# A decoder layer on one core: two feed-forward chunks by seven products, and more weight remainders by transfer

## The chip, the cores and the metric

The kernel runs on one NeuronCore of a Trainium2 chip. The metric is device time in microseconds (us) of one execution. TensorE (PE, with its weight loads as PEld), VectorE (DVE), ScalarE (ACT), GpSimd (POOL) and SyncE (SP) each run their own list of instructions in the order written. They wait for each other through semaphores. SP, ACT and POOL can issue DMA transfers.

## The reference

One decoder layer on 256 tokens of width 1024, in float32. The part that the change touches is the last one, with D_FF = 2816:

```
def swiglu(h, w_gate, w_up, w_down):
    return (jax.nn.silu(h @ w_gate) * (h @ w_up)) @ w_down
...
        mix = jnp.concatenate([pool_out, attn_out], axis=-1) @ w_out[l]
        h = layer_norm(DEEPNORM_ALPHA * h + mix, ln1_g[l], ln1_b[l])
        h = layer_norm(DEEPNORM_ALPHA * h + memory_cross_attention(h, mem, w_xq[l], w_xkv[l], w_xo[l]),
                       ln2_g[l], ln2_b[l])
        h = layer_norm(DEEPNORM_ALPHA * h + swiglu(h, w_gate, w_up, w_down), ln3_g[l], ln3_b[l])
```

## The kernel before

**Numbers in two parts.** A float32 operand is held as a high part (rounded to TensorE's reduced float32) and a low part (the rest). A product of two operands is three matmuls: high x high, high x low, low x high (`three`). A weight tile of 128 x 1024 numbers (0.524 MB) is loaded by SP into a raw page. ACT casts the high part from it, and DVE subtracts to get the low part (`split`). For a tile named in `BY_DMA`, `parted` does otherwise: ACT writes the negated high part into the low page, and POOL issues a DMA that adds the weight from DRAM onto it. Names such as w63 are weight tiles in the order of their making; r, h and l behind a name are raw, high and low.

**Stages.** The layer runs through input projections, attention and pooling, keys of the memory (xk), the output projection (mix), the values of the memory (xv), the queries (xq), the output of the cross attention (xo), gate and up (gu), down (d), and the last norm. DFF is cut into 11 chunks of 256 columns. Chunk 0 is formed in rows: the token rows stand on the partitions, 48 matmuls of 512 columns, then SiLU and product, then four transposes. Chunks 1 to 10 are formed the other way round (`proj_both`): 32 matmuls of 512 columns and 32 of 256, and the result needs no transpose. `gated` adds the two accumulators, applies SiLU and product, splits the result and, for the down stage, forms four sums of its quarters (`add_sums`) and splits these.

**Seven products instead of eight.** `Blocks.seven` multiplies a 256 x 256 operand by a 256 x 1024 weight in seven block products rather than eight, from the quarters and four sums of quarters on both sides. That is 21 matmuls of 512 columns, three for each of the seven. The sums of the weight's quarters are made in one of three ways, which a letter names. 'D' loads both rows and adds on DVE (`FromVector`). 'S' adds in DRAM ahead of time: copies and adds by DMA into sumt, mixt or xot, then loads of the sums (`FromDram`). 'A' loads two quarters and lets POOL add two others onto them in SBUF by DMA, and DVE adds the other two sums (`FromAdded`). A weight pair has tiles o (the first quarter, shared by two pairs), y (two quarters), z and w (two sums each). `MIX`, `XO` and `DOWN` give the letter of each pair of a stage. The sums take the bank accumulators 1 to 7; `joined` and the adds behind it put the four output quarters together. `several` and `DEFER` put the last pairs' last three products at the end.

**The order.** `Plan.schedule` fixes the order of every engine before the program is built. TensorE's order is the order of the code. The others are filled by deadlines worked back from TensorE's nominal times, with a model of durations and of the transfer queue. Tiles take slots: 42 pages of 4 KB per partition, 4 big ones, 8 halves. A load may be issued only when a slot is free, and `MARGIN`, `SPARE`, `RAWS` say how far ahead slots may be taken. `LEAVE` is the time after which a bank should be empty, `PATIENCE` how long an engine may hold back for a more urgent operation. `XV_STEPS` and `XA_STEPS` say after how many products of xv, xq and xo the transposes and attention steps stand. `transpose_tok` transposes half a row of tokens and splits it into h1T or h2T, the operands of the next stage. `APART` says, for each half of token block 0 in the last norm, whether ACT and POOL scale it (`scale_apart`) or DVE (`scale`).

## Time and profile before

| what | value |
|---|---|
| median of 3 runs | 371.98 us (371.61 to 373.33) |
| the profiled execution | 373.54 us, of which the span 371.6 us |
| PE busy | 363.6 us, 98% of the span |
| DVE busy | 320.2 us, 86% |
| ACT busy | 242.6 us, 65% |
| POOL busy | 38.2 us, 10% |
| DMA moved | 95.26 MB, 256 GB/s over the span |

The span reaches from the first to the last instruction of the profiled execution. Busy is the time in which an engine has an instruction under way. A matmul's duration overlaps that of the next one, so what a product costs is read from the distance of starts, not from its duration. The same holds, by less, for passes of DVE. The DMA share in the windows is the mean busy share of 16 DMA engines; it can be a little over 1 since packets overlap.

### The profile page before, as it was taken

What the parts mean: (1) busy time and instruction counts of PE and PEld (TensorE: products, weight loads), DVE (VectorE), ACT (ScalarE), POOL (GpSimd) and SP (SyncE); (2) the same over time, 40 slices, a digit from 0 to 9 for tenths busy, and PEclk for the clock granted to TensorE, in tenths of its full rate; (3) what the DMA queues carried; (4) which work ended last, traced back from release to release, by engine and by line L of the source; (5) the groups of instructions that cost most, each with busy time, mean ns of one, the idle gap of its engine ahead of it and who ended that gap; (6) DMA issues with size and microseconds to landing.
All of it is one profiled execution on the core that took longest, in us unless ns stands there. A gap on an engine that the chain in (4) does not pass through costs nothing. (4 is left out here: it accounts for less than half of the span.)

```text
span 371.6 us, 5494 instructions
## 1 busy us (share of the span) xinstructions
PE 363.6 (98%) x1971; PEld 310.9 (84%) x1971; DVE 320.2 (86%) x489; ACT 242.6 (65%) x364; POOL 38.2 (10%) x43
## 2 busy tenths in 40 slices
...
GB/s 225 415 417 416 335 305 300 82 196 197 305 408 353 201 220 297 52 304 323 330 319 372 284 278 361 294 259 181 221 275 59 217 95 227 282 267 417 52 0 113
DMA packets 34059, 95.26 MB, mean 256 GB/s; under 512 B 3440, under 2 KB 5488, under 8 KB 34032
## 3 DMA queue, kind: packets, MB, share of 16 engines
...
q0 software_dynamic: 6688, 12.85, 20.1%
...
q10 hardware_dynamic: 288, 0.33, 0.2%
...
## 5 line engine op out<-in xcount | busy, mean ns | idle before, releaser
L528 DVE TENSOR_TENSOR sg<-banks,sg 128x512 f32<-128x512 f32 x20 | 12.9, 685 | 14.9 <-ACT sg L510 14.9
L510 ACT COPY sg<-banks 128x512 f32<-128x512 f32 x20 | 10.7, 587 | 18.7 <-PE banks L571 18.7
L1362 POOL TENSOR_TENSOR rs<-rs,mhalf 128x1 f32<-128x1 f32 x6 | 5.6, 930 | 46.9 <-DVE rs L542 46.9
L533 DVE SCALAR_TENSOR_TENSOR r<-r,mv,g 128x512 f32<-128x512 f32 (+2 forms) x12 | 8.3, 720 | 0.0
L533 DVE SCALAR_TENSOR_TENSOR r<-r,rs,b 128x512 f32<-128x512 f32 (+1 forms) x10 | 6.8, 707 | 1.3 <-POOL rs L1362 1.2
L1350 DVE BATCH_NORM_STATS2 st<-r 128x6 f32<-128x512 f32 (+1 forms) x12 | 7.7, 665 | 0.2
L518 ACT ACTIVATE xpr<-banks,mx 128x256 f32<-128x256 f32 x8 | 3.7, 470 | 6.4 <-DVE mx L890 6.4
L559 POOL DMA_DIRECT2D sumt<-in_s_down x4 | 4.2, 1040 | 35.1 <-DMA sumt<-in_s_down 35.1
L528 DVE TENSOR_TENSOR sg<-sg 128x512 f32<-128x512 f32 x10 | 6.8, 685 | 0.7 <-ACT sg L518 0.7
L518 ACT ACTIVATE sg<-sg 128x512 f32<-128x512 f32 x10 | 6.4, 635 | 1.3 <-DVE sg L528 1.3
L518 ACT ACTIVATE pr<-pr,mx 128x128 f32<-128x128 f32 (+1 forms) x16 | 7.1, 451 | 0.0
L528 DVE TENSOR_TENSOR r<-banks,r 128x512 f32<-128x512 f32 (+1 forms) x11 | 7.0, 655 | 0.0
L510 ACT CAST rest<-r 128x256 fp32r<-128x256 f32 x1 | 0.4, 407 | 9.6 <-DVE r L528 9.6
L559 POOL DMA_DIRECT2D mixt<-in_s_out x2 | 2.5, 1240 | 38.9 <-DMA mixt<-in_s_out 38.9
L518 ACT ACTIVATE pr<-pr,sm 128x256 f32<-128x256 f32 (+1 forms) x16 | 5.8, 447 | 0.0
L576 PEld LDWEIGHTS banks<-ident,r 128*128 128x128 f32 x32 | 3.9, 140 | 1.5 <-DVE r L533 0.6
L576 PE MATMUL banks<-ident,r 128*128 128x128 f32 x32 | 4.8, 273 | 0.2 <-DVE r L533 0.2
L533 DVE SCALAR_TENSOR_TENSOR xql<-banks,xq 128x512 f32<-128x512 f32 x4 | 2.8, 690 | 2.5 <-ACT xq L518 2.5
L913 DVE CUSTOM_DVE_ANT_0 pr<-banks,tri 128x128 f32<-128x128 f32 (+1 forms) x16 | 4.7, 352 | 0.2
L510 ACT CAST h1T<-banks 128x512 fp32r<-128x512 f32 x4 | 2.3, 587 | 3.8 <-PE banks L576 3.8
L518 ACT ACTIVATE xq<-banks 128x512 fp32r<-128x512 f32 x4 | 2.4, 593 | 3.7 <-PE banks L571 3.7
L559 POOL DMA_DIRECT2D w47l<-in_w_gu x1 | 1.2, 1237 | 30.8 <-ACT w47l L518 30.8
...
## 6 DMA issues: line engine op xcount, KB each, us to landing
...
mixt<-in_s_out SPq DMA_DIRECT2D x3, 512.0 KB, 8.9
g<-in_ln_g SPq DMA_DIRECT2D x3, 512.0 KB, 7.4
b<-in_ln_b SPq DMA_DIRECT2D x3, 512.0 KB, 7.3
...
mr<-in_mem_t SPq DMA_DIRECT2D x2, 512.0 KB, 10.5
mixt<-in_s_out POOLq DMA_DIRECT2D x2, 512.0 KB, 12.7
xt<-in_x SPq DMA_DIRECT2D x2, 512.0 KB, 4.2
```

The source lines that it names most:

```text
L510: return self.add(eng, lambda: f(out.ap(), src.ap()), out, [src], 1, **kw)
L518: nc.scalar.activation(out.ap(), src.ap(), func, bias=val(bias), scale=val(scale), **more)
L528: return self.add(eng, lambda: e.tensor_tensor(out.ap(), a.ap(), b.ap(), op=op), out, [a, b], 2, **kw)
L533: return self.add(eng, lambda: e.scalar_tensor_tensor(out.ap(), a.ap(), val(scalar), b.ap(), op0=op0, op1=op1), out, [a, b, scalar], 2, **kw)
L559: return self.plan.op("POOL", lambda: self.nc.gpsimd.dma_start(val(out), val(src), accum_op=OP.add, max_dma_last_dim=2048), [out], [src], ...
L576: return self.plan.op("PE", lambda: self.nc.tensor.transpose(ps.ap(), src.ap(), ident.ap()), [ps], [src, ident], 0.109, DRAIN, kind=False)
L913: nc.vector.tensor_tensor_reduce(o.ap(), i.ap(), tri.ap()[:, S - w:], -1.0, -NEG, op0=OP.add, op1=OP.min, accum_out=m.ap())
L1350: plan.op("DVE", lambda: nc.vector.bn_stats(st.ap(), r.ap()), [st], [r], *kit.cost("DVE", c1 - c0))
L1362: plan.op("POOL", lambda: nc.gpsimd.tensor_tensor(rs.ap(), rs.ap(), mhalf.ap(), op=OP.pow), [rs], [rs, mhalf], 0.83, 0.05)
```

## The change

The change forms chunks 4 and 5 of gate and up together (`group`, step 'G0' of `SEQUENCE`): their 512 gate and 512 up columns are one weight of 1024 x 1024, four pairs of 256 rows, each in seven products by the way 'A', with sums of h2's quarters on the other side. For these `transpose_tok` keeps a raw copy of h2T (h2raw, two pages, copied by ACT), and `form_of_h2` makes and splits the sums (hs). The result comes out in rows, and is transposed. Chunk 6 is formed in rows (step 'R6'), and the eight transposes of chunks 4 and 5 stand in it; its own four stand in chunk 7. `gated_t` now also forms the sums of quarters from a copy.

In the other stages the letters D of the mix and S of xo and down become A, so that nothing of down and xo is added in DRAM any more. `BY_DMA` lists thirty names instead of nine. The second half of token block 0 in the last norm goes to DVE. The planner gets other constants and, in its model of the transfers, a list of times at which SP's queue is held up; `XV_STEPS`, `XA_STEPS` and `IN_BIG` change. Of the new code's `AHEAD` nothing runs, since it is 0. The core of the diff:

```diff
-LEAVE = 3.0
-PATIENCE = 0.7
-MARGIN, SPARE, RAWS = 100.0, 1, 6
+LEAVE = 2.0
+PATIENCE = 1.0
+MARGIN, SPARE, RAWS = 40.0, 1, 5
 BEHIND = 1.35
 RING = 256
-ADD_LATE = 6.0, 100.0
+AHEAD = 0.0
+FETCHES = 18.9, 43.5, 62.5, 82.0, 110.0, 137.0, 154.0, 179.5, 205.0, 226.5, 248.0, 268.5, 290.0, 313.0, 343.5
+ADD_LATE = (6.0, 100.0)
...
-MIX = ('D', 'D', 'S', 'S')
+MIX = ('A', 'A', 'S', 'S')
 VAL = ('', '', '', '')
-XO = ('D', 'S', '', '')
-DOWN = {1: 'A', 2: 'A', 3: 'S', 4: 'S', 5: 'A', 6: 'A', 7: 'S', 8: 'S', 9: 'A'}
+XO = ('D', 'A', '', '')
+DOWN = {1: 'A', 2: 'A', 3: 'A', 4: 'A', 5: 'A', 6: 'A', 7: 'A', 8: 'A', 9: 'A'}
 LAST = tuple(c for c in range(NFC) if c not in DOWN)
-BY_DMA = ('w27', 'w28', 'w29', 'w36', 'w47', 'w49', 'w52', 'w56', 'w59')
-DEFER = (1, 2)
-APART, HALF_STORES = (True, True), True
-IN_BIG = ('g1', 'g2')
+BY_DMA = ('d4o', 'd6o', 'd7y', 'd8o', 'd8y', 'gu0y', 'gu1y', 'gu2y', 'w27', 'w28', 'w30', 'w33', 'w36', 'w37', 'w47', 'w49', 'w52', 'w57', 'w61', 'w73', 'w75', 'w78', 'w81', 'w83', 'w88', 'w91', 'w93', 'w95', 'xo1o', 'xo1y')
+DEFER = (1, 2, 1)
+GROUPS = ((4, 5),)
+TURN_AT = (1, 2)
+SEQUENCE = (1, 2, 3, 'G0', 'R6', 7, 8, 9, 10)
+APART, HALF_STORES = (True, False), True
+IN_BIG = ('g1', 'g3')
...
-XV_STEPS = 16, 4
-XA_STEPS = ((21, 's0'), (34, 'p0'), (35, 's1'), (52, 'p1'), (52, 's2'), (53, 'a0'), (59, 'a1'), (61, 'p2'), (69, 's3'), (73, 'a2'), (77, 'p3'))
+XV_STEPS = (12, 6)
+XA_STEPS = ((21, 's0'), (34, 'p0'), (37, 's1'), (53, 's2'), (53, 'a0'), (56, 'p1'), (58, 'p2'), (60, 'a1'), (68, 's3'), (75, 'a2'), (77, 'p3'))
...
-        split(*gated_parts(0), pt.re("p f (t s) -> p (f t) s", t=T))
+                kit.transpose(pt[:, f, t * P:(t + 1) * P], rows_[t][:, f * P:(f + 1) * P], ident)
+        q = pt.re("p f (t s) -> p (f t) s", t=T)
+        hl = gated_parts(c)
+        if c not in LAST:
+            raw = half("sg", [4, P], hold=12)
+            copy("ACT", raw, q)
+            q = raw
+            add_sums((hl[0][:, 4:8], hl[1][:, 4:8]), q)
+        split(hl[0][:, 0:4], hl[1][:, 0:4], q)
...
+            three(ps, h2T.pair(k, slice(t * P, (t + 1) * P)), c_gu[c].get(k), k == 0, k == KD - 1)
             yield
+    h2_sums = {}
+    def form_of_h2(j):
+        if j not in h2_sums:
+            v = h2_sums[j] = page(f"hs{j}", [2, 4, P], F32R)
+            add_sums((v[:, 0], v[:, 1]),
+                     h2raw[j // 2][:, 2 * (j % 2):2 * (j % 2) + 2, :].re("p k (t s) -> p (k t) s", t=T))
+        def get(f):
+            if f < 4:
+                return h2T.pair(2 * j + f // 2, slice(f % 2 * P, (f % 2 + 1) * P))
+            return h2_sums[j][:, 0, f - 4], h2_sums[j][:, 1, f - 4]
+        return get
+    gu_sums = DramSums("gu", s_gu, y_gu, 4 * len(GROUPS), 0) if GROUPS else None
+    def group(n):
+        b = Blocks("gm")
+        yield from b.several([(form_of_h2(j), FromAdded(f"gu{4 * n + j}", gu_sums, 4 * n + j), "A", 0) for j in range(4)],
+                             DEFER[2], ORDERS, None)
+        m1, u2, u3 = b.joined()
+        g = [half("gr", [512], hold=12) for _ in range(2)]
+        u = [half("ur", [512], hold=8) for _ in range(2)]
+        tt("DVE", g[0], b.m[2], m1, OP.add)
+        tt("DVE", u[0], b.m[5], u2, OP.subtract)
+        tt("DVE", u[1], b.m[5], u3, OP.subtract)
+        tt("DVE", u[0], b.m[3], u[0], OP.add)
+        tt("DVE", g[1], b.m[4], u3, OP.add)
+        for y, z in zip(g, u):
+            act(y, y, AF.Silu)
+            tt("DVE", y, y, z, OP.mult)
+        turned.extend((c, [y[:, i * CW:(i + 1) * CW] for y in g]) for i, c in enumerate(GROUPS[n]))
...
+    for at, c in enumerate(SEQUENCE, 1):
         mark = [plan.pe[-1]]
-        if c <= len(thirds):
-            down_sums.begin(thirds[c - 1], mark)
-        if c == 3:
+        if at <= len(thirds):
+            down_sums.begin(thirds[at - 1], mark)
+        if at == 3:
             for js in thirds:
                 down_sums.add(js, mark)
-        gu = proj_both(pss + more, c_gu[c], h2T, KD if c < NFC - 3 else 2)
-        if c == 1:
-            run(gu, 8)
-            gated_t()
-        run(gu)
-        gated(c, gate, up)
+        if isinstance(c, str) and c[0] == "G":
+            g = group(int(c[1:]))
+            if turned:
+                run(g, 4)
+                turn()
+            run(g)
+        elif isinstance(c, str):
+            c = int(c[1:])
+            before = list(turned)
+            turned.clear()
+            for t in range(T):
+                row = bank("pg")
+                g = rows_of(c, t, row)
+                if t == TURN_AT[0]:
+                    run(g, TURN_AT[1])
+                    for other, rows_ in before:
+                        gated_t(other, rows_)
+                run(g)
+                gated_row(c, t, row)
+            turned.append((c, [sg_rows[c][:, t, :] for t in range(T)]))
+        else:
+            gate, pss = two("pg")
+            up, more = two("pu")
+            gu = proj_both(pss + more, c_gu[c], h2T, KD if at < len(SEQUENCE) - 2 else 2)
+            if turned:
+                run(gu, 8)
+                turn()
+            run(gu)
+            gated(c, gate, up)
+    turn()
```

On TensorE, at the place of chunk 4, this is the order before: eight products of each weight tile with h2T, high parts first.

```order
L571 MATMUL banks<-h2T_2050,w62l 128x256 x8
L571 MATMUL banks<-h2T_2032,w63h 128x512 x8
L571 MATMUL banks<-h2T_2032,w64h 128x512 x8
L571 MATMUL banks<-h2T_2050,w65h 128x512 x8
L571 MATMUL banks<-h2T_2050,w66h 128x512 x8
L571 MATMUL banks<-h2T_2032,w63l 128x256 x8
L571 MATMUL banks<-h2T_2032,w64l 128x256 x8
```

At the same place after: the group's tiles gu0y, gu0o, gu0z and gu0w against quarters of h2T and their sums hs.

```order
L600 MATMUL banks<-h2T_2043,w62l 128x256 x8
L600 MATMUL banks<-gu0yh,h2T_2019 128x512
L600 MATMUL banks<-gu0yl,h2T_2019 128x512
L600 MATMUL banks<-gu0yh,h2T_2019 128x512
L600 MATMUL banks<-gu0yh,hs_2234 128x512
L600 MATMUL banks<-gu0yl,hs_2234 128x512
L600 MATMUL banks<-gu0yh,hs_2234 128x512
L600 MATMUL banks<-gu0oh,h2T_2019 128x512
L600 MATMUL banks<-gu0ol,h2T_2019 128x512
L600 MATMUL banks<-gu0oh,h2T_2019 128x512
L600 MATMUL banks<-gu0zh,hs_2234 128x512
```

The two chunks' 64 matmuls each are replaced by 84 of 512 columns, every one in three behind the tiles of its pair.

On VectorE, around the sums of chunk 3's product (sg), the order before: low parts of later weight tiles between.

```order
L528 TENSOR_TENSOR w76l<-w76r,w76h 128x1024
L528 TENSOR_TENSOR sums<-sg 128x256
L528 TENSOR_TENSOR g3l<-sg,g3h 128x512
L528 TENSOR_TENSOR sums<-sums,sg 128x128
L528 TENSOR_TENSOR w77l<-w77r,w77h 128x1024
L528 TENSOR_TENSOR sums<-sg,sums 128x128
L528 TENSOR_TENSOR w78l<-w78r,w78h 128x1024
L528 TENSOR_TENSOR w79l<-w79r,w79h 128x1024
```

At the same place after:

```order
L557 TENSOR_TENSOR gu3w<-gu3y,gu3z 128x512
L557 TENSOR_TENSOR sums<-sg 128x256
L557 TENSOR_TENSOR gu3w<-gu3y,gu3w 128x512
L557 TENSOR_TENSOR sums<-sums,sg 128x128
L557 TENSOR_TENSOR sums<-h2raw_2047 128x256
L557 TENSOR_TENSOR g_2534<-sg,g_2534 128x512
L557 TENSOR_TENSOR sums<-sg,sums 128x128
L557 TENSOR_TENSOR sums<-sums,h2raw_2047 128x128
L557 TENSOR_TENSOR gu3zl<-gu3z,gu3zh 128x1024
L557 TENSOR_TENSOR sums<-h2raw_2047,sums 128x128
L557 TENSOR_TENSOR gu3wl<-gu3w,gu3wh 128x1024
L557 TENSOR_TENSOR gu3yl<-gu3y,gu3yh 128x1024
```

Where low parts of tiles four chunks ahead stood, the group's last tiles are made ready, and the first of these rows needs POOL's add into gu3z.

On POOL, the adds for the down stage before (the other sums came from DRAM, added earlier into sumt):

```order
L559 DMA sumt_101<-sumt_100 128x512
L559 DMA d1z<-in_s_down 128x2x512
L559 DMA d2z<-in_s_down 128x2x512
L559 DMA d5z<-in_s_down 128x2x512
L559 DMA d6z<-in_s_down 128x2x512
L559 DMA d9z<-in_s_down 128x2x512
```

And after, nine sums and three low parts (yl, w83l) of the same stage:

```order
L588 DMA d1z<-in_s_down 128x2x512
L588 DMA d2z<-in_s_down 128x2x512
L588 DMA d3z<-in_s_down 128x2x512
L588 DMA d4z<-in_s_down 128x2x512
L588 DMA d5z<-in_s_down 128x2x512
L588 DMA d6z<-in_s_down 128x2x512
L588 DMA d7z<-in_s_down 128x2x512
L588 DMA d7yl<-in_y_down 128x2x512
L588 DMA d8z<-in_s_down 128x2x512
L588 DMA d9z<-in_s_down 128x2x512
L588 DMA d8yl<-in_y_down 128x2x512
L588 DMA w83l<-in_w_down 128x2x512
```

All adds of the stage now stand in a row on POOL's one queue, each behind the load or cast that it adds onto.

## Rows read from the trace of the kernel before

**Rows 1.** The span of the core and its mean granted clock.
```profile
core 0: 371.6 us, clock 0.995
```

**Rows 2.** Windows: length, PE, PEld, DVE, ACT, POOL busy (instructions), clock, DMA share, GB/s.
```profile
24.00:34.00 10.00, 9.60 (x58) 7.66 (x57) 9.48 (x20) 9.48 (x15) 0.00 (x0) 1.00 1.03 419
...
156.00:198.00 42.00, 41.85 (x220) 35.08 (x220) 40.03 (x63) 34.88 (x50) 8.06 (x7) 1.00 1.03 313
198.00:242.00 44.00, 44.00 (x257) 38.77 (x256) 36.55 (x47) 26.29 (x34) 6.29 (x6) 1.00 1.06 320
242.00:300.00 58.00, 58.00 (x334) 50.92 (x333) 42.34 (x63) 32.14 (x46) 3.62 (x3) 1.00 0.68 194
300.00:346.00 46.00, 46.00 (x220) 38.61 (x219) 40.45 (x47) 31.96 (x35) 2.41 (x2) 1.00 0.81 268
```

**Rows 3.** Timeline of PE, chunk 4: start, length, line, operation, tiles, shape, count.
```profile
231.07 2.00 PE L571 MATMUL banks<-h2T,w63h 128*128 128x512 f32 x8
...
238.40 1.12 PE L571 MATMUL banks<-h2T,w63l 128*128 128x256 f32 x8
...
242.21 0.39 PE L571 MATMUL banks<-h2T,w67h 128*128 128x512 f32 x1
```

**Rows 4.** The longest wait of PE: for whom, total, times, longest.
```profile
PE banks L571 <- ACT diag L518: 1.4, 1, 1.4
```

**Rows 5.** Timeline of PE, down stage, first matmul of chunk 3 and of chunk 4.
```profile
318.75 0.39 PE L571 MATMUL banks<-d3yh,g3h 128*128 128x512 f32 x1
...
323.51 0.39 PE L571 MATMUL banks<-d4yh,g4h 128*128 128x512 f32 x1
```

**Rows 6.** Timeline of PE, chunk 0 in rows, from tile w48 to its end.
```profile
193.04 0.40 PE L571 MATMUL banks<-w48h,h2T 128*128 128x512 f32 x1
...
197.21 0.62 PE L571 MATMUL banks<-h2T,w51h 128*128 128x512 f32 x2
```

**Rows 7.** Timeline of PE, the transposes of chunk 0's product.
```profile
204.55 0.60 PE L576 MATMUL banks<-ident,sg 128*128 128x128 f32 x4
204.90 1.20 PE L571 MATMUL banks<-h2T,w51l 128*128 128x256 f32 x8
205.94 1.12 PE L571 MATMUL banks<-h2T,w52l 128*128 128x256 f32 x8
```

**Rows 8.** Timelines of PE and DVE at the first transposes of h1.
```profile
114.69 0.60 PE L576 MATMUL banks<-ident,r 128*128 128x128 f32 x4
...
111.27 0.75 DVE L533 SCALAR_TENSOR_TENSOR r<-r,rs,b 128x512 f32<-128x512 f32 x1 [0.80 <-POOL rs L1362]
```

**Rows 9.** Timelines of POOL and DVE in the tail.
```profile
362.32 2.52 POOL L528 TENSOR_TENSOR r<-r,b 128x512 f32<-128x512 f32 x2 [0.83 <-ACT r L518]
...
364.42 0.43 DVE L1350 BATCH_NORM_STATS2 st<-banks 128x6 f32<-128x256 f32 x1 [0.58 <-PE banks L571]
```

**Rows 10.** Timeline of DVE, passes of 1024, 512 and 256 with their successors.
```profile
198.17 1.22 DVE L528 TENSOR_TENSOR w58l<-w58r,w58h 128x1024 fp32r<-128x1024 f32 x1
199.30 1.22 DVE L528 TENSOR_TENSOR w60l<-w60r,w60h 128x1024 fp32r<-128x1024 f32 x1
...
206.11 0.68 DVE L528 TENSOR_TENSOR go<-banks,go 128x512 fp32r<-128x512 f32 x1
206.71 1.21 DVE L528 TENSOR_TENSOR w66l<-w66r,w66h 128x1024 fp32r<-128x1024 f32 x1
...
237.02 0.41 DVE L528 TENSOR_TENSOR sums<-sg 128x256 f32<-128x256 f32 x1
237.35 0.68 DVE L528 TENSOR_TENSOR g3l<-sg,g3h 128x512 fp32r<-128x512 f32 x1
```

**Rows 11.** The DMA queue of POOL: packets, MB, share of 16 engines' span.
```profile
q0 software_dynamic: 6688, 12.85, 20.1%
```

**Rows 12.** DMA issues, one add of POOL: count, size, us to landing.
```profile
d1z<-in_s_down POOLq DMA_DIRECT2D x1, 512.0 KB, 7.1
```

**Rows 13.** Timeline of PE, first matmul with the last weight tile.
```profile
355.02 0.39 PE L571 MATMUL banks<-w94h,go 128*128 128x512 f32 x1
```

82 lines of the change are left out of this document (59 added, 23 removed).

## The prediction

> **What bounds the kernel now.** I first read the span and clock of the core [rows 1]: 371.6 us, granted clock 0.995, so nothing here is throttled. Then the windows [rows 2]: TensorE is busy for every microsecond of 198 to 346, and for 41.85 of the 42 before it. Busy alone proves little, since matmuls overlap, so I read the spacing of their starts: one chunk of gate and up, 32 products of 512 columns and 32 of 256, goes from 231.07 to 242.21 [rows 3], which is 0.229 us a wide product and 0.119 a narrow one, with no pause between them. The list of TensorE's waits agrees: the longest in the whole span is 1.4 us, in the tail [rows 4]. So between the start and the tail the time is the number of products times their spacing. A product that goes is time saved, and an operand that comes late is time lost. The other engines and the DMA queue have room only because they run ahead.
>
> **What the change removes and adds on TensorE.** Durations are those of the profiled execution, span 371.6 us. It took 373.54 us as a whole, so 1.94 us lie around the span, and it stands 1.56 us above the median of the runs (371.98). I work out a difference of spans and take it from the median.
>
> - Chunks 4 and 5 leave the old form: 2 x 11.14 = 22.28 us gone [rows 3]. So does chunk 6: 11.14 us gone.
> - The group comes: 4 pairs x 7 products x 3 matmuls of 512 columns = 84. The down stage runs that same form: 21 matmuls from 318.75 to 323.51 [rows 5], 0.2267 us each, so 19.04 us. A slower row exists: with transposes near, chunk 0 in rows took 4.17 us for 18 matmuls, from 193.04 to 197.21 [rows 6], 0.2317 each, so 19.46 us. The group has no transposes in it: I take 19.04.
> - Chunk 6 in rows: 48 matmuls of 512. Eight transposes stand between them, so I take the slower spacing: 11.12 us (10.88 by the faster).
> - Twelve transposes more: eight for chunks 4 and 5, four for chunk 6. Four took 0.35 us, and the products behind them 1.20 where their like took 1.12 [rows 7]: 0.43 for a group of four, 0.78 for the eight that go as one, together 1.21 us.
>
> Sum: 19.04 + 11.12 + 1.21 - 33.42 = -2.05 us; with all low ends -2.29, with all high ends -1.63.
>
> **What it moves elsewhere.**
>
> - The transposes of h1 stand after 12 instead of 16 products of the value projection, 12 matmuls or 2.7 us before 114.69 where they start now, so at 112.0. The half row that they read is written from 111.27, for 0.75 us [rows 8], so ready at 112.0. VectorE has less to do ahead of it (two pairs of the mix no longer form their sums there). Cost 0 to 0.7 us, I take 0.
> - In the tail the second half of token 0 is scaled by VectorE instead of by ScalarE and GpSimd. It is a pass of at most 0.75 us [rows 8], put in ahead of a measurement that waits 0.58 us for TensorE now [rows 9]; so it costs 0.17 us at most, and I take 0.1. The lower end is a gain: GpSimd's two adds, 2.52 us in all, become one. Range -0.3 to +0.7.
> - Of the thirty names for low parts by transfer, eight name tiles that the program never makes (d4o, d6o, d8o, xo1o, w88, w91, w93, w95); 22 take effect, 9 before. Each takes one pass of 1.13 us from VectorE and puts one more pass on ScalarE and one add on GpSimd's queue. VectorE gives back most of that: the order has 8 x 128 more, 6 x 256 more, 11 x 512 more, 6 x 1024 fewer passes. It stays near its present load, and its place in time is what matters.
>
> **VectorE in the group.** In the new order, between the first pass after chunk 0's second product (at 198.17) and the last operand form of the group (hs3), stand 15 passes of 1024, 27 of 512 and 21 small ones. A pass of 1024 takes 1.13 us, one of 512 0.60, a small one at most 0.33, by the starts of neighbours [rows 10]: 17.0 + 16.2 + 6.9 = 40.1 us, so 238.3 if it never waits. TensorE asks for hs3 after three pairs and one product, 66 matmuls past 231.07: at 246.0. The cushion is 7.7 us. In the stretch 198 to 242 VectorE now stands idle for 44 - 36.55 = 7.45 us [rows 2], so the same idleness would just fit. There is a new wait in this order: gu3w stands ahead of gu3zl and needs the add into gu3z. Behind it are queued the halves of chunk 3's product, the low parts of gu3 and of w63 to w65, and then the seven passes that empty the group's banks, for which the rows of chunk 6 wait.
>
> **The DMA queue.** Loads alone move 419 GB/s, loads with adds between them 313 to 320 [rows 2]; a load of 0.524 MB is thus 1.25 us. The adds moved 12.85 MB in 20.1% of the span [rows 11], 74.7 us, or 3.05 us for 0.524 MB. From 156 us, where the queue starts afresh, the new order has 79 loads to the last weight and 28 adds: 98.8 + 85.4 = 184 us, against 86 loads and adds of 16 such sizes before, 156 us.
>
> - To the add of gu3z it is 29.5 loads and 12 adds, 73.5 us, so 229.5. Then some 4 us until it lands (one add took 7.1 us from issue to landing [rows 12], 3.05 of it transfer), two passes of 512 and two of 1024 at most: 237. Against 246.0 that leaves 9 us.
> - To the end it is 340.2, and 346.6 with landing and two passes. TensorE asks for the last weight tile (w94 before, w86 now) at 355.02 [rows 13] less 2, at 353. That leaves 6.4 us. Here the cover is thin: now the queue idles for 0.32 x 58 + 0.19 x 46 = 27 us between 242 and 346 [rows 2].
>
> The price of an add decides, and the rows have adds slow: 3.05 us. The Trainium skill (DMA: Bandwidth & Descriptors, section Anatomy of one DMA — SWDGE (gpsimd) path) gives 2.0 us plus bytes over 436 GB/s for a transfer from GpSimd's queue, an estimate of 1.2 us of engine time for an add; by it the 28 adds would be 34 us and the cushion at the end 58 us. The 7.1 us of the trace speak against it. The Trainium skill (DMA: Bandwidth & Descriptors, section SWDGE vs HWDGE vs iDMA) says that an engine takes its queues in turn, so that adds don't run beside loads but between them; the fall from 419 to 320 GB/s agrees, and if they ran beside, the cushions would be larger by 37 and 85 us.
>
> **The forecast.** No wait outlives its cushion: -2.05 + 0.1 = -1.95 us, 371.98 - 1.95 = 370.0 us. Its own range is 369.3 (all low ends) to 371.0 (all high ends with the 0.7 of one moved step).
>
> **The rivals.**
>
> - **Slower: the transfers become the bound in the down stage.** Place: the y, z and last weight tiles behind 300 us. For it: 184 us of transfer in the 190 from 156 to 346, nine adds in the down stage where there were five, and a queue that has idled for lack of free slots. Against it: it idled because it was far ahead. It decides when the queue loses over 6.4 us from 156 on; every further microsecond is a microsecond of TensorE. Idle for half of the 27 us is 13.7, a wait of 7.3 and 377.3 us; for 11.4 us, a wait of 5 and 375 us, which I take.
> - **VectorE is late in the group.** If it waits for gu3z's add on top of its 7.45 us idle, the cushion of 7.7 is overdrawn by the 2 or so that the add may come later: 372.0 us, no difference.
> - **More is gained.** The small waits before the tail [rows 4] shrink as VectorE is relieved ahead of the norms, and the low ends hold: -2.29 - 0.7 = -3, 369.0 us.
>
> **How the numbers follow.** Forecast 0.50, VectorE late 0.20, transfers the bound 0.22, more gained 0.08. The measurement can tell about 0.5% (1.86 us) from no change, so the line of faster is 370.1. Of the forecast's 0.50 some 0.30 lie below that line, 0.20 above it; the third rival is faster; VectorE late is the same but for 0.03; of the transfers' 0.22 some 0.20 are slower. Faster 0.38, same 0.39, slower 0.23. The range reaches from 369.0 to 375.5, which leaves out the far half of the slow rival and a little below.
>
> **What would show it.** In the new profile: the group's 84 matmuls in 19.0 to 19.5 us without a step; no wait of TensorE over 0.5 us between 112 and 360, above all none for gu3's tiles, at the transposes of h1, or for d and w83 to w86 tiles; VectorE's wait ahead of gu3w short; the DMA share over 0.9 from 156 to 340. Wrong would be a wait for a z tile or a last weight tile, which makes it the first rival, or a spacing of the group over 0.232 us.

## The result, and the profile after

The changed kernel takes **377.0 us** (median of 5 runs, 375.6 to 377.6) where the kernel before takes 372.51 (5 runs, 371.61 to 373.33). The ratio is 1.0115, interval 1.0086 to 1.0145. It is slower, and it lies above the range of the prediction. The profiled execution of after took 376.33 us, its span is 374.6 us, 3.0 us over the span in [rows 1]. These two profiles show 3.0 of the 4.5 us between the medians: the profiled execution of before lies 1.0 us above its median, that of after 0.7 below. The rest has no row.

Windows of after (length, busy time of PE, PEld, DVE, ACT and POOL, clock, DMA share, GB/s), to be read against [rows 2]:

```profile
198.00:242.00 44.00, 44.00 (x242) 38.22 (x241) 37.74 (x63) 30.96 (x42) 6.08 (x5) 1.00 0.92 241
242.00:300.00 58.00, 58.00 (x310) 49.68 (x309) 49.87 (x72) 40.18 (x55) 10.87 (x9) 1.00 1.01 287
300.00:346.00 46.00, 42.86 (x195) 34.42 (x194) 37.66 (x46) 30.96 (x35) 8.48 (x7) 1.00 0.95 260
```

TensorE is still full up to 300. In the last window, where it was busy for all of 46 us, it now lacks 3.1 us, and the DMA share is 0.95 instead of 0.81. The waits of TensorE from 190 us on (for whom, total, times, longest) name the place:

```profile
PE banks L600 <- ACT diag L547: 1.4, 1, 1.4
PE banks L600 <- ACT d5wh L539: 1.4, 1, 1.4
PE banks L600 <- DVE d8wl L557: 1.0, 1, 1.0
PE banks L600 <- DVE d5wl L557: 0.9, 1, 0.9
PE banks L600 <- DVE d6wl L557: 0.8, 1, 0.8
```

The first was there before [rows 4]. The four of the down stage are new. TensorE's timeline with its milestones (start, length, line, tiles, shape, count, idle time before):

```profile
230.91 0.39 PE L600 MATMUL banks<-gu0yh,h2T 128*128 128x512 f32 x1
...
250.16 0.39 PE L600 MATMUL banks<-w63h,h2T 128*128 128x512 f32 x1
...
262.13 0.86 PE L600 MATMUL banks<-h2T,w67h 128*128 128x512 f32 x3
...
273.71 0.85 PE L600 MATMUL banks<-h2T,w71h 128*128 128x512 f32 x3
...
307.28 0.40 PE L600 MATMUL banks<-d1yh,g 128*128 128x512 f32 x1
...
326.35 0.39 PE L600 MATMUL banks<-d5yh,g5h 128*128 128x512 f32 x1
...
331.31 0.50 PE L600 MATMUL banks<-d5wh,g5h 128*128 128x512 f32 x1 [1.40 <-ACT d5wh L539]
...
346.93 0.50 PE L600 MATMUL banks<-d8wl,g8h 128*128 128x512 f32 x1 [0.97 <-DVE d8wl L557]
...
354.60 0.39 PE L600 MATMUL banks<-w83h,go 128*128 128x512 f32 x1
```

The kernel before passed the same places at these times:

```profile
309.19 0.40 PE L571 MATMUL banks<-d1yh,g 128*128 128x512 f32 x1
...
328.27 0.39 PE L571 MATMUL banks<-d5yh,g5h 128*128 128x512 f32 x1
...
350.77 0.39 PE L571 MATMUL banks<-w91h,go 128*128 128x512 f32 x1
```

The account, after less before. The start of the group against that of chunk 4 [rows 3]: -0.16. From there to the down stage 76.37 instead of 78.12: -1.75. From d1yh to d5yh 19.07 instead of 19.08: nothing. From d5yh to the first of the last weight tiles 28.25 instead of 22.50: **+5.75**. From there to the end of the span 20.00 instead of 20.83: -0.83. The sum is +3.0.

The starts that stand further apart than 0.2275 us add up to 5.65 us behind d5yh: 2.9 at d5w, 1.3 at d6w, 1.2 at d8w, 0.2 at d9w. So nearly the whole loss is that the w forms of the last pairs come late. Why are they late? ScalarE's timeline, after:

```profile
329.27 1.05 ACT L539 CAST d6yh<-d6y 128x1024 fp32r<-128x1024 f32 x1 [6.65 <-DMA d6y<-in_y_down]
330.22 1.04 ACT L539 CAST d5wh<-d5w 128x1024 fp32r<-128x1024 f32 x1
...
332.12 1.04 ACT L539 CAST d8yh<-d8y 128x1024 fp32r<-128x1024 f32 x1
...
334.45 1.05 ACT L539 CAST w83h<-w83r 128x1024 fp32r<-128x1024 f32 x1 [0.19 <-DMA w83r<-in_w_down]
...
336.50 1.04 ACT L539 CAST d6wh<-d6w 128x1024 fp32r<-128x1024 f32 x1
```

And the same place before:

```profile
323.97 1.05 ACT L510 CAST d6yh<-d6y 128x1024 fp32r<-128x1024 f32 x1 [0.49 <-DMA d6y<-in_y_down]
324.98 1.06 ACT L510 CAST d5wh<-d5w 128x1024 fp32r<-128x1024 f32 x1
```

The order d6yh, d5wh is the same in both kernels. What differs is the wait ahead of it: ScalarE stands for 6.65 us until d6y has landed, and d5wh, whose data VectorE had written by 324.8, stands behind it. VectorE waits too, and the casts of d8y and w83, which TensorE asks for some 20 us later, stand ahead of d6wh:

```profile
324.13 0.69 DVE L557 TENSOR_TENSOR d5w<-d5y,d5w 128x512 f32<-128x512 f32 x1
...
330.35 1.23 DVE L557 TENSOR_TENSOR d6yl<-d6y,d6yh 128x1024 fp32r<-128x1024 f32 x1 [4.40 <-ACT d6yh L539]
...
337.57 1.23 DVE L557 TENSOR_TENSOR d6wl<-d6w,d6wh 128x1024 fp32r<-128x1024 f32 x1 [1.92 <-ACT d6wh L539]
```

Was d6y issued late? No: SP issued it at 317.28, before at 317.07. It took longer to land, 329.18 instead of 323.87. Its cushion shrank by more than these 5.3 us, since TensorE starts d5yh 1.9 us earlier than before and so asks for d6y earlier. The DMA issues from 312 to 350 (KB, us from issue to landing), after:

```profile
d7z<-in_s_down POOLq DMA_DIRECT2D x1, 512.0 KB, 8.7
...
d6y<-in_y_down SPq DMA_DIRECT2D x1, 512.0 KB, 11.9
d7yl<-in_y_down POOLq DMA_DIRECT2D x1, 512.0 KB, 11.2
d8z<-in_s_down POOLq DMA_DIRECT2D x1, 512.0 KB, 15.5
```

And before:

```profile
d6y<-in_y_down SPq DMA_DIRECT2D x1, 512.0 KB, 6.8
```

After, GpSimd issued three adds at 314.92, 318.29 and 319.02, around d6y, and SP issued d8z, a tile needed much later, ahead of it. Before, GpSimd's one add of these 38 us came at 323.27. And VectorE can't make good what it loses. The kernel before has this window from 326 to 354 (columns as above):

```profile
326.00:354.00 28.00, 28.00 (x124) 22.95 (x123) 25.89 (x29) 16.10 (x18) 0.00 (x0) 1.00 0.67 240
```

VectorE is busy for 25.89 of the 28 us there; 2.1 us are to spare. In the changed kernel it is busy for 21.59 of them. The two waits above, 4.40 and 1.92 us, are most of what is missing, and behind the second, from 337.57 to 351.6, its passes follow each other with no wait, while TensorE waits for d6wl and d8wl. The reading to be tested is thus: a tile that lands 5 us later, a fixed order behind it, and an engine that has no room once it is behind.

### The profile page after: what moved, and what is told of

It reads as the page before. It is cut to its first block, busy times and chain, and to the rows that moved or that the text cites. A ratio compares the mean times of both kernels' runs of the same rounds, so it can differ in the third digit from the quotient of the medians.

```text
span 374.6 us, 5464 instructions
## 1 busy us (share of the span) xinstructions
PE 363.1 (97%) x1923; PEld 306.1 (82%) x1923; DVE 325.7 (87%) x509; ACT 261.8 (70%) x388; POOL 57.6 (15%) x57
## 3 DMA queue, kind: packets, MB, share of 16 engines
q0 software_dynamic: 11152, 21.50, 32.3%
## 4 chain that ended last, share of the span: by engine, by line
PE 85%; DMA 5%; DVE 4%; ACT 2%; issue 1%; SPq 1%; DVEq 0%; ACTq 0%
PE banks L600 83%; DMA w83r<-in_w_down 3%; PE banks L605 2%; DMA w7r<-in_w_qkv 2%; SPq L583 1%; DVE r L562 1%; ACT xpr L547 0%; DVE d8w L557 0%; DVE d4wl L557 0%; DVE d8wl L557 0%; DVE d5yl L557 0%; DVE d7zl L557 0%; ACT d5yh L539 0%; ACT w83h L539 0%; ACT d6wh L539 0%
## 5 line engine op out<-in xcount | busy, mean ns | idle before, releaser
L539 ACT COPY sg<-banks 128x512 f32<-128x512 f32 x17 | 9.2, 588 | 14.1 <-PE banks L600 10.2
L557 DVE TENSOR_TENSOR sg<-banks,sg 128x512 f32<-128x512 f32 x14 | 9.0, 686 | 7.5 <-ACT sg L539 7.5
L562 DVE SCALAR_TENSOR_TENSOR r<-r,rs,b 128x512 f32<-128x512 f32 (+1 forms) x11 | 7.6, 709 | 0.6 <-POOL rs L1398 0.5
L588 POOL DMA_DIRECT2D w73l<-in_w_gu x1 | 1.2, 1203 | 34.3 <-DVE ur L557 34.3
L539 ACT CAST d6yh<-d6y 128x1024 fp32r<-128x1024 f32 x1 | 1.0, 1046 | 6.6 <-DMA d6y<-in_y_down 6.6
L588 POOL DMA_DIRECT2D w27l<-in_w_xkv x1 | 1.2, 1197 | 28.6 <-PE banks L600 28.6
L557 DVE TENSOR_TENSOR sums<-sg 128x256 f32<-128x256 f32 x9 | 3.7, 422 | 1.9 <-ACT sg L539 1.8
L557 DVE TENSOR_TENSOR d6yl<-d6y,d6yh 128x1024 fp32r<-128x1024 f32 x1 | 1.2, 1225 | 4.4 <-ACT d6yh L539 4.4
L539 ACT CAST h2T<-banks 128x512 fp32r<-128x512 f32 x4 | 2.4, 594 | 3.5 <-PE banks L605 3.5
```

The lines of the kernel that those rows point to most:

```text
L539: return self.add(eng, lambda: f(out.ap(), src.ap()), out, [src], 1, **kw)
L557: return self.add(eng, lambda: e.tensor_tensor(out.ap(), a.ap(), b.ap(), op=op), out, [a, b], 2, **kw)
L562: return self.add(eng, lambda: e.scalar_tensor_tensor(out.ap(), a.ap(), val(scalar), b.ap(), op0=op0, op1=op1), out, [a, b, scalar], 2, **kw)
L588: return self.plan.op("POOL", lambda: self.nc.gpsimd.dma_start(val(out), val(src), accum_op=OP.add, max_dma_last_dim=2048), [out], [src], ...
```

## The experiments

In the diffs, a row such as ('ACT', 'd6yh', 'ACT', 'd5wh') takes ScalarE's pass that writes d6yh out of the order and puts it right behind the one that writes d5wh. Each ratio is to the kernel before on the same chip, with its 95% interval. "The stretch" is that from the first product with d1yh to the first with the last weight tiles: 41.58 us before, 47.32 after.

### Is it the order alone?

**d6yh and d6yl behind the passes of d5w.**

```diff
+            ('ACT', 'd6yh', 'ACT', 'd5wh'),
+            ('DVE', 'd6yl', 'DVE', 'd5wl'),
```

> The changed kernel with one place of two written orders exchanged: on ScalarE the cast d6yh stands behind d5wh instead of ahead of it, on VectorE d6yl behind d5wl. Transfers and TensorE's list are untouched. In the changed kernel ScalarE stood idle for 6.65 us ahead of d6yh (until d6y landed at 329.2), while d5w had been ready since 324.8 and d5wh stood behind; TensorE lost 1.55 and 1.22 us at d5z/d5w. Theory A (the written order is what costs: one late tile holds up others that are ready): the 2.8 us at d5w go and about 0.3 us at d6y comes, so 374.5 us against 377.0. Theory B (the transfers are late as such, 28 adds among them, and whatever stands first waits): the wait moves to d6y and d6w, whose casts stay behind w83h, and under 1 us is won: 376.2 us.

377.35 us, 1.0142 (1.0121 to 1.0162): nothing gained. The waits for d5w are gone, and TensorE waits one pair later, for d6wh, which stands behind ScalarE's casts of d6y, d8y and w83:

```profile
337.96 0.50 PE L600 MATMUL banks<-d6wh,g6h 128*128 128x512 f32 x1 [2.67 <-ACT d6wh L539]
339.22 0.80 PE L600 MATMUL banks<-d6wl,g6h 128*128 128x512 f32 x1 [0.76 <-DVE d6wl L557]
339.81 0.63 PE L600 MATMUL banks<-d6wh,g6l 128*128 128x512 f32 x1
340.24 0.63 PE L600 MATMUL banks<-d6wh,g6h 128*128 128x512 f32 x1
```

These rows show a second loss. Behind the two waits the starts stand 0.43 us apart instead of 0.23, and the granted clock from 339.4 to 341.6 is 0.50, the lower of its two levels (1.2 instead of 2.4 GHz); by 342.4 it is back at 1.00. The waits come to some 4.5 us of the stretch, 1.2 less than in the changed kernel, and the lower clock costs another 1.3. The waits of the changed kernel, 1.40 and 0.95 us, left its clock at 1.00.

**Six more passes that are not urgent moved back.**

```diff
+            ('ACT', 'd8yh', 'ACT', 'd6wh'),
+            ('ACT', 'd8yl', 'ACT', 'd8yh'),
+            ('POOL', 'd8yl', 'ACT', 'd8yl'),
+            ('ACT', 'w83h', 'ACT', 'd7zh'),
+            ('ACT', 'w83l', 'ACT', 'w83h'),
+            ('POOL', 'w83l', 'ACT', 'w83l'),
```

> As the kernel with d6yh behind d5wh, and moreover ScalarE's passes for the low parts by transfer of d8y (d8yh, d8yl) stand behind d6wh and those of w83 (w83h, w83l) behind d7zh, with their adds behind them. In the changed kernel d6wh was cast at 336.5, after four such passes of which one waited for w83 to land at 334.4, though d6w was complete at 335.1. Theory A (the written order costs): of the 5.7 us that the down stage lost about 4 go, 373 us. Theory B (the transfers are late as such): d6y lands at 329 and d8y, d9y, d7o with 12 to 14 us from issue to landing as before; d6w, d7 and d8 go on waiting, and the two adds that now start later come late for d8y and w83: 375.5 us or more.

376.74 us, 1.0132 (1.0097 to 1.0167). Now ScalarE is in time and VectorE isn't: five waits, for d6wl 0.8, d7zl 0.8, d7wl 0.5, d7ol 0.4 and d8wl 1.1, 3.6 us in all. The clock stays at 1.00, and the starts lose 5.8 us in the stretch, as much as in the changed kernel. The order alone decides who is waited for, and hardly how long. That the order alone is to blame is refuted.

### Which part of the change does it?

**The group taken out, the rest kept.**

```diff
-GROUPS = ((4, 5),)
+GROUPS = ()
-SEQUENCE = (1, 2, 3, 'G0', 'R6', 7, 8, 9, 10)
+SEQUENCE = tuple(range(1, 11))
```

> The changed kernel with chunks 4 to 6 of gate and up formed as before (no group, no chunk 6 in rows); the letters A of the down stage, the low parts by transfer and all else stay as changed, the order is planned anew. Theory B1 (the loss sits in the down stage and has nothing to do with the group): TensorE gets back the 1.75 us that chunk 4 to the start of the down stage had won (230.91 to 307.28, against 231.07 to 309.19), the down stage keeps its 5.7 us: 378.8 us. Theory B2 (the group's four pairs, with four adds and nine pages, set the transfers back and this reaches the down stage): the waits there shrink by over 3 us, 375.5 us or less.

377.62 us, 1.0139 (1.0114 to 1.0164). The stretch takes 47.30 us, with the group 47.32. ScalarE again waits 5.7 us for d6y. The group has no share in the loss of the stretch. What it gains shows ahead of it: d1yh starts at 308.57 here, 1.3 us later than with the group.

**The kernel before with the letters A in the down stage, nothing else.**

```diff
-DOWN = {1: 'A', 2: 'A', 3: 'S', 4: 'S', 5: 'A', 6: 'A', 7: 'S', 8: 'S', 9: 'A'}
+DOWN = {1: 'A', 2: 'A', 3: 'A', 4: 'A', 5: 'A', 6: 'A', 7: 'A', 8: 'A', 9: 'A'}
```

> The kernel before with one edit: the four letters S of the down stage become A, as in the change. Theory B (adds in the down stage are too many by themselves): four adds more behind 275 us, and waits of 2 us or more there: 374.5 us. Theory B3 (it takes the low parts by transfer as well, d7y, d8y and w83 to w81 among them): the idle third of the queue between 242 and 320 takes the four adds, no wait: 372.2 us.

376.54 us, 1.0103 (1.0082 to 1.0125): the letters alone, without the group, cost most of what the change costs. Not all of it is in one place: the stretch takes 44.80 us, 3.2 more than before where the change has 5.7 more, and from the last weight tiles to the end it is 0.8 us longer than before. The waits of TensorE, the landing of d6y, and the windows (columns as above):

```profile
PE banks L571 <- DVE d8wl L528: 1.1, 1, 1.1
PE banks L571 <- DVE d7wl L528: 0.8, 1, 0.8
```

```profile
d6y<-in_y_down SPq DMA_DIRECT2D x1, 512.0 KB, 10.1
```

```profile
198.00:242.00 44.00, 44.00 (x258) 38.82 (x257) 35.68 (x46) 27.00 (x37) 0.00 (x0) 1.00 0.59 199
242.00:300.00 58.00, 58.00 (x335) 51.00 (x334) 41.18 (x61) 31.54 (x45) 6.02 (x5) 1.00 0.75 205
```

Here the queue is idle for 0.41 x 44 + 0.25 x 58 = 32.5 us between 198 and 300, and 3.2 us are lost all the same. So this much does not need more bytes from 156 us on than there is time for. The adds meet the loads in one stretch, behind 312. The letters also give VectorE two passes of 512 more between 326 and 354, for d7w and d8w: by the 0.60 us of [rows 10] 1.2 of the 2.1 us that it had to spare. How the other 2.5 us of the stretch divide between the low parts by transfer, the planner's new constants and the rest of the change was not tested.

**The letters of before in the changed kernel.**

```diff
-DOWN = {1: 'A', 2: 'A', 3: 'A', 4: 'A', 5: 'A', 6: 'A', 7: 'A', 8: 'A', 9: 'A'}
+DOWN = {1: 'A', 2: 'A', 3: 'S', 4: 'S', 5: 'A', 6: 'A', 7: 'S', 8: 'S', 9: 'A'}
```

> The changed kernel with the letters of the down stage as before (pairs 3, 4, 7, 8 by sums made in DRAM between 180 and 245), group and all else as changed, planned anew. Theory B (the four adds that the letters A put behind 275 us are what is too much there): four loads of 1.25 us for each pair in place of three loads and an add of 3.05, with the two sums' loads that makes about 2.2 us less a pair, 2 to 4 of the 5.7 us go: 374 us. Rival D (what the letters S need, 8 copies and 8 adds in DRAM, now stands in front of the group's own loads): TensorE waits for gu tiles from 231 on, or for the sums in the down stage: 378 us or more.

384.86 us, 1.0331 (1.0308 to 1.0355), the worst of all. The group takes 26.75 us instead of 19.25; the longest waits are those for its last pair:

```profile
PE banks L600 <- ACT gu3wh L539: 2.6, 1, 2.6
...
PE banks L600 <- DVE gu3wl L557: 1.0, 1, 1.0
```

With the sums formed in DRAM during gate and up, the group's own tiles come late. Behind these waits the granted clock is 0.50 from 252.8 to 256, so part of the group's 7.5 us is the clock. Nor does the stretch get better by the old letters: it takes 47.91 us, though d6y landed 4.7 us after its issue there, and TensorE waits for d4wl, d5wl, d7wl, d8wl and d8zl instead. So in the changed kernel the letters A are not what has to go; whether another plan could carry the letters S was not tested.

### Is it the number of adds?

**Three adds left out, the order kept** (the low parts of d7y, d8y and w83 then lack the weight itself).

```diff
+    for o in plan.order:
+        if o.eng == "POOL" and o.bufs and o.bufs[0].name in ("d7yl", "d8yl", "w83l"):
+            o.fn = lambda: None
```

> The changed kernel in its own order, but the three transfers that add d7y, d8y and w83 onto their low parts are left out, so the low parts of these three tiles are wrong. Every pass and every load stays where it is. Theory B (too much transfer between 314 and 348): 3 adds of 3.05 us are 9.15 us less for the queue, of which one add lies ahead of d6y's landing; d6y lands some 3 us earlier, at 326, d6wh comes in time, and at least 4 of the 5.7 us go: 373 us or less. Theory A (the written order): ScalarE waits for d6y as before unless it lands by 322, so at most the part that comes from an earlier landing goes: 375.5 us.

375.11 us, 1.0081 (1.0066 to 1.0096). d6y takes 10.5 us to land instead of 11.9, and the stretch 45.67 us: 1.65 of the 5.75 us are gone for three adds.

**The same three tiles taken out of the list, order replanned.**

```diff
-BY_DMA = ('d4o', 'd6o', 'd7y', 'd8o', 'd8y', 'gu0y', 'gu1y', 'gu2y', 'w27', 'w28', 'w30', 'w33', 'w36', 'w37', 'w47', 'w49', 'w52', 'w57', 'w61', 'w73', 'w75', 'w78', 'w81', 'w83', 'w88', 'w91', 'w93', 'w95', 'xo1o', 'xo1y')
+BY_DMA = ('d4o', 'd6o', 'd8o', 'gu0y', 'gu1y', 'gu2y', 'w27', 'w28', 'w30', 'w33', 'w36', 'w37', 'w47', 'w49', 'w52', 'w57', 'w61', 'w73', 'w75', 'w78', 'w81', 'w88', 'w91', 'w93', 'w95', 'xo1o', 'xo1y')
```

> The changed kernel without d7y, d8y and w83 in the list of low parts by transfer: VectorE subtracts these three (3 passes of 1.13 us, in a stretch 320 to 346 where it is busy 19.1 of 26 us), three adds and three passes of ScalarE go, and the order is planned anew. Theory B (too much transfer): all waits of the down stage go but for 1 us, 371.5 us. Theory A (the written order): depends on the place that d6yh gets; if ahead of d5wh again, 375 us. Rival C (VectorE needs the relief that these three adds give): the waits come back as waits for VectorE's subtractions, 377 us or more.

374.9 us, 1.0076 (1.0047 to 1.0104). In its profile the stretch takes 42.27 us, nearly that of before. The new plan also issues d6y 1.6 us earlier, so this is not the adds alone. But VectorE has three passes more, and the tail loses 1.7 us against before: 22.56 us from the last weight tiles to the end. TensorE waits 2.5 instead of 1.4 us for diag, and behind that wait the clock is 0.50: the last two products take 1.65 us where before they took 0.91.

**And with token block 0 scaled as before.**

```diff
-APART, HALF_STORES = (True, False), True
+APART, HALF_STORES = (True, True), True
```

> The changed kernel without d7y, d8y and w83 among the low parts by transfer (374.9 us, of which the tail from the first w83 product to the end took 22.56 us in the profiled run, against 20.83 before), and with both halves of token block 0 scaled by ScalarE and GpSimd again. Theory C (with three subtractions more VectorE is what ends the tail): two passes of 0.7 us leave VectorE, the tail shortens by 1 to 1.7 us: 373.5 us. If TensorE or the norm's chain ends it: 374.9 us, no change.

376.34 us, 1.0102 (1.0068 to 1.0135), against the expectation: the tail didn't get shorter, since the scaling stood late in the new order all the same. It showed another thing. SP's and GpSimd's lists of the down stage have the order of the kernel just shown, and d6y landed 8.0 us after its issue there, 10.5 here; d8wl, waited for 0.2 us there, was waited for 1.1 here. The stretch takes 43.90 us. Such a stage stands on the edge: with the same lists a landing decides how long the waits are.

### Is it the landing of d6y?

**The kernel before, d6y issued later** (behind d7y and d7o; the engines' order untouched but for d6yh, which can't stand ahead of its load).

```diff
+    for early, late in (("d6y", "d7y"),):
+        early, late = loads[early], loads[late]
...
+        order[i], order[j] = late, early
+    for o, behind in ((at["SP", "d6y"], at["SP", "d7o"]), (at["ACT", "d6yh"], at["SP", "d6y"])):
+        order.remove(o)
+        order.insert(order.index(behind) + 1, o)
```

> The kernel before with one edit in SyncE's list: d6y is issued behind d7y and d7o instead of ahead of them (its page exchanged with d7y's), so that it lands near 330.5 instead of 323.9, about where it landed in the changed kernel (329.2). Nothing is added or left out, the other lists stay. Theory E (a tile of the down stage that lands 6 us late costs TensorE most of that, since d5w is queued behind it on two engines and VectorE has no room to make it up): waits at d5w and behind, 375.5 us. Theory B (only the amount of transfer counts): the same amount, 372.5 us, no change.

377.1 us, 1.0132 (1.0108 to 1.0157). No add, no letter and no group was touched, and by the medians one load that lands 5.0 us later costs about what the change costs. ScalarE waits for it as in after, and TensorE waits first at the same pair:

```profile
328.94 1.05 ACT L510 CAST d6yh<-d6y 128x1024 fp32r<-128x1024 f32 x1 [6.09 <-DMA d6y<-in_y_down]
329.90 1.04 ACT L510 CAST d5wh<-d5w 128x1024 fp32r<-128x1024 f32 x1
```

```profile
PE banks L571 <- DVE d5wl L528: 0.9, 1, 0.9
...
PE banks L571 <- DVE d6wl L528: 0.2, 1, 0.2
```

The profiled execution was the shortest of the four, 375.42 us, and its rows show less: the stretch takes 43.54 us, 1.96 more than before and not 5.74, with no wait for d5wh and none at d8w. So the trace shows that a late d6y alone brings back the first of the waits. That it alone costs as much as the change rests on the medians. The two longest executions (377.69 and 378.01 us) have a mean granted clock of 0.991, the others 0.996 and 0.998; how much of their loss is waits and how much a lower clock is shown by no trace.

**The changed kernel, the loads of d6y and d8z exchanged.**

```diff
+    for early, late in (("d8z", "d6y"),):
+        early, late = loads[early], loads[late]
...
+        order[i], order[j] = late, early
```

> The changed kernel with nothing but the loads of d6y and d8z exchanged in SyncE's list (pages too). The four passes moved on ScalarE alone gave 376.7 us, both together 373.3. Theory E1 (the late landing of d6y alone is the cause): 373.5 us. Theory E2 (both are needed, since d6wh stands behind passes that wait for w83 and d8y): d5w's waits go, but d6wh waits for w83, which lands near 332 to 334: 375 us.

374.52 us, 1.005 (1.0031 to 1.0069): d6y lands 5.2 us after an issue that is 4.5 us earlier, the waits for d5w are gone, and those for d6wh (1.5) and d6wl (0.8) remain, behind the casts of d8y and w83. Behind them the clock falls here too, 0.51 from 338 to 341, which costs 1.6 of the 4.4 us that the stretch of this execution still loses. **With the six passes moved back as well:**

```diff
+    for early, late in (("d8z", "d6y"),):
...
+            ('ACT', 'd8yh', 'ACT', 'd6wh'),
+            ('ACT', 'd8yl', 'ACT', 'd8yh'),
+            ('POOL', 'd8yl', 'ACT', 'd8yl'),
+            ('ACT', 'w83h', 'ACT', 'd7zh'),
+            ('ACT', 'w83l', 'ACT', 'w83h'),
+            ('POOL', 'w83l', 'ACT', 'w83l'),
```

> The changed kernel with the loads of d6y and d8z exchanged in SyncE's list (their pages too), so that d6y is issued near 313 instead of 317.3, ahead of most adds; and the four passes of ScalarE for the low parts of d8y and w83 behind d6wh and d7zh, as in the run that moved them alone and won nothing. Number and size of all transfers stay. Theory E (one tile that lands late, and two engines whose written order stands behind it, make the loss; VectorE, idle 4.4 us ahead of d6yl, has no room to make it up): d6y lands near 319, the waits at d5w and d6w (about 4 us) go, 373 us. Theory B (28 adds are too much for the queue, whatever comes first): d8z and its add come that much later, the waits move to d8, and 376 to 377 us remain.

373.31 us, 1.0022 (1.001 to 1.0034). By the ratios one load issued some 4 us earlier takes back 2.4 of some 4.3 us, the order another 1.0. The order that gained nothing while d6y was late gains something once it isn't. In the profiles that is more the clock, which stays at 1.00 here, than the waits: the starts still lose 2.4 us in the stretch, and the stretch takes 44.02 us. That the ratio is near 1 all the same is the group's gain ahead of it and a tail 0.9 us shorter than before.

### Is there an order in which the change pays?

**The exchange, the three tiles out of the list, and a scaling pass earlier in the tail.**

```diff
+    for early, late in (("d8z", "d6y"),):
...
+    order.remove(scale)
+    order.insert(at + 1, scale)
```

> The changed kernel without d7y, d8y and w83 among the low parts by transfer (374.9 us by itself, 372.1 of span in its profiled run), with the loads of d6y and d8z exchanged (pages too), and in the last norm VectorE's first scaling pass of token block 0 right behind its mean and variance instead of three passes later. Theory E: d6y lands before 320 in every run, no wait in the down stage but for 0.5 us at d8w; in the tail GpSimd has the first half of block 0 done before it is asked for block 1, which gives back about 1.1 of the 1.75 us that its tail was longer: 371.5 us, level with before or better. If VectorE is the bound in both places (it works without a pause from 327 to 359 in that kernel): 374 us.

377.35 us, 1.0128 (1.0111 to 1.0144). The tail became shorter, 20.89 us, and the wait moved on: ScalarE now stands for tiles whose adds are late. TensorE waits 2.6 us for d8wh and 0.8 for d8wl, the clock behind that is 0.50 from 345.6 to 348.4, and the stretch is 47.28 us again. With the three tiles out of the list the exchange of the loads did harm.

```profile
336.19 1.06 ACT L539 CAST d8zh<-d8z 128x1024 fp32r<-128x1024 f32 x1 [4.61 <-DMA d8z<-in_s_down]
341.23 1.04 ACT L539 CAST d9zh<-d9z 128x1024 fp32r<-128x1024 f32 x1 [3.04 <-DMA d9z<-in_s_down]
```

**The exchange, only w83 out of the list, and the passes of pairs 6 to 9 in the order in which TensorE asks.**

```diff
+        ('ACT', 'd7zh', 'ACT', 'd6zh'),
+        ('ACT', 'd8yl', 'ACT', 'd6wh'),
+        ('ACT', 'd7wh', 'ACT', 'd8yl'),
+        ('DVE', 'd7zl', 'DVE', 'd6wl'),
+        ('DVE', 'd9w 0', 'DVE', 'd8wl'),
...
+        ('ACT', 'w83h', 'ACT', 'd9zh'),
```

> The changed kernel with the loads of d6y and d8z exchanged (that exchange, with four passes of ScalarE moved, gave 373.3 us, of which 2.4 us are still lost in the down stage, at d7w, d8w and d9w); w83 no longer among the low parts by transfer; on ScalarE and VectorE the passes of pairs 6 to 9 in the order in which TensorE asks for them, where their inputs have landed (d7zh, d6wh and d7wh ahead of d7oh, d8yl behind d6wh, w83h last, d9w behind d8wl); both scaling passes of token block 0 in the last norm right behind its variance. All operands and the group stay as in the change. Theory E (late tiles and the order behind them are all that the down stage loses): under 1 us of waits remains, 371.6 us, ahead of before by some 0.3%. Rival (with the letters A VectorE has too many passes from 327 on, whatever the order): 373 us, no better than the exchange alone.

378.76 us, 1.0176 (1.0147 to 1.0205), a clear miss. SP issued w83 to w86 at 330.0 to 332.5 (in the changed kernel w83 at 321.8, w84 to w86 at 335.5 to 336.4), loads that TensorE asks for behind 350, and the adds issued in the same 5 us landed late:

```profile
d9z<-in_s_down POOLq DMA_DIRECT2D x1, 512.0 KB, 14.3
...
d8yl<-in_y_down POOLq DMA_DIRECT2D x1, 512.0 KB, 15.3
```

d9z landed at 345.03, and TensorE waited for d8wh 1.5, d8wl 0.8, d9wl 0.8 and d9wh 0.4 us. Between them the clock was 0.50 from 345.6 to 348, which costs another 1.3 us.

**Against this miss: the load of w84 held back** (it is given d9w's page, so that it can't start before 335.8), d8y out of the list instead of w83, the exchange kept, the passes in asking order.

```diff
-BY_DMA = ('d4o', 'd6o', 'd7y', 'd8o', 'd8y', 'gu0y', 'gu1y', 'gu2y', 'w27', 'w28', 'w30', 'w33', 'w36', 'w37', 'w47', 'w49', 'w52', 'w57', 'w61', 'w73', 'w75', 'w78', 'w81', 'w83', 'w88', 'w91', 'w93', 'w95', 'xo1o', 'xo1y')
+BY_DMA = ('d4o', 'd6o', 'd7y', 'd8o', 'gu0y', 'gu1y', 'gu2y', 'w27', 'w28', 'w30', 'w33', 'w36', 'w37', 'w47', 'w49', 'w52', 'w57', 'w61', 'w73', 'w75', 'w78', 'w81', 'w83', 'w88', 'w91', 'w93', 'w95', 'xo1o', 'xo1y')
...
+    for a, b in (("w84r", "d9w"),):
+        a, b = [next(f for o in order for f in o.bufs if f.name == n) for n in (a, b)]
+        a.slot, b.slot = b.slot, a.slot
```

> The changed kernel with d6y's load exchanged with d8z's, d8y no longer among the low parts by transfer (one add and one pass of ScalarE less, one subtraction of VectorE more, late), the passes of pairs 6 to 9 on ScalarE and VectorE in the order in which TensorE asks, both scaling passes of token block 0 in the last norm early, and the loads of w84 to w86 held back: w84 takes the page of d6wl, which TensorE lets go near 336. In the run that lost most (378.8 us) these three loads were issued from 331 on instead of 337, and the adds of d8z and d9z took 10.0 and 14.3 us to land instead of 6.9 and 9.1. Theory F (the landing of the tiles that are asked for next is what counts, and it is set by what else was issued before them): d8z lands before 337, d9z before 340, waits under 1 us in the down stage, 371.6 us. Rival G (VectorE has too many passes from 327 on for the letters A): at least 2 us of waits at d8w and d9w again, 373.3 us or more.

373.1 us, 1.0019 (1.0007 to 1.003). The stretch takes 41.78 us, with no wait in it, and the clock stays at 1.00. The adds into the same tiles land sooner than in the miss, which has as many adds:

```profile
d8z<-in_s_down POOLq DMA_DIRECT2D x1, 512.0 KB, 7.1
d9z<-in_s_down POOLq DMA_DIRECT2D x1, 512.0 KB, 9.0
```

VectorE has one pass more than in the changed kernel and is in time. So it wasn't that VectorE had too much to do in this stage; it had been kept waiting, and could not make it good. Several edits stand in this kernel together, and what each of them is worth was not parted. **The same with w84l and w85l earlier on VectorE and the last scaling pass ahead of the last measurement:**

```diff
+        ('DVE', 'w84l', 'DVE', 'd9yl'),
+        ('DVE', 'w85l', 'DVE', 'w84l'),
...
+    order.remove(last)
+    order.insert(order.index(acc), last)
```

> As the third candidate (373.1 us; down stage 41.78 us, without a wait; tail 21.86 us from the first w83 product to the end, where before has 20.83), with four passes of VectorE moved in the tail: w84l and w85l ahead of the emptying of the banks, where VectorE was idle for 0.78 us, and the last pass of token block 0 ahead of the last measurement, where it was idle for 0.58 us. If the tail loses by VectorE's order: the 0.3 us wait for w84l goes, the last three passes become two (0.6 us), 372.2 us, level with before. If the tail is bound by something else: 373.1 us.

372.29 us against 372.40 of before, ratio 0.9999 (0.9989 to 1.0009): level. The change can be had without its loss, and then it gains nothing that the runs show. In its profile, span 370.7, TensorE reaches the down stage 1.58 us earlier than in the profile of before and ends 0.9 us earlier. That the medians are level has to do with the profile of before, whose 373.54 us stand 1.1 above the 372.40. Where an ordinary execution of before is quicker than the profiled one is shown by no trace, and so it stays open what became of the microsecond and a half.

## Why the prediction was wrong, point by point

- **The sum on TensorE held.** From the group's start to the down stage -1.75 where -2.05 was forecast, within its bounds of -1.63 to -2.29. The group took 19.25 us (0.2292 a matmul, between the 0.2267 and 0.2317 of [rows 5, 6]) against 19.04, and that is 0.21 of the 0.3. Chunk 6 with the eight transposes in it took 11.97, against 11.12 + 0.78 = 11.90; chunk 7 with four 11.58, against 11.14 + 0.43 = 11.57.
- **The moved steps held.** The first transposes of h1 start at 110.92 without a wait, so they cost nothing. In the tail, from the product with b to the end it is 7.37 us in both kernels: 0 where 0.1 was taken. That the stretch ahead of it became 0.83 us shorter was not foreseen; VectorE, ahead of a delayed TensorE, no longer lets it wait for r.
- **VectorE late in the group didn't come.** TensorE has no wait between 198 and 307. The cushions were enough, but smaller than forecast: the sums hs3 were written at 243.55 and not at 238.3, so 2.5 of the 7.7 us were left.
- **The step that failed is the DMA queue's second one**, "To the end it is 340.2, and 346.6 with landing and two passes." As a sum of volume it was not far off: the queue was busy for 0.92, 1.01 and 0.95 of the windows from 198 to 346, as the part on what would show it asked, and the last of these transfers, the add into w83l, landed at 349.86, ahead of the 354.83 at which TensorE took it; the sum's 340.2 and its 4 us of landing would make it 344.2. But it asked only about the last tile. The cushion of each tile on the way was never worked out, and d6y had none: asked for near 331 (21 products behind d5yh), landed at 329.18, with two passes behind it and the passes of d5w in line behind those. The wait stood some 20 us ahead of the place that the sum looked at.
- **The price of an add in time was taken from one row.** The 7.1 us to landing of [rows 12] is an add with no other add beside it. With up to three under way and loads between, it was 8.7 to 15.5 us behind 312, and the load of d6y beside them took 11.9 instead of 6.8. In engine time the price was right. GpSimd's queue, after (packets, MB, share of 16 engines' span):

```profile
q0 software_dynamic: 11152, 21.50, 32.3%
```

  These are 41 such tiles in 32.3% of 374.6 us, 2.95 us each, near the 3.05 of [rows 11]. The Trainium skill (DMA: Bandwidth & Descriptors, section Anatomy of one DMA — SWDGE (gpsimd) path) gives 2.0 us plus bytes over 436 GB/s, an estimate of 1.2 us for the data of such a tile and 3.2 us to its landing. The traces do not agree with it for adds, with 2.95 us of the engines and at least 7.1 us to landing in the rows above.
- **The first rival was right in place and nearly in size.** It put the loss in the down stage, at y and z tiles, and 5 us of wait; the rows show 5.65, at the w tiles that stand in line behind a late y tile. Its mechanism was half right. It wanted a queue that lost over 6.4 us somewhere behind 156, so that the last tile comes late. The kernel with the letters alone has a queue that idles for 32.5 us and still loses 3.2 us in the stretch. What it takes is a tile that lands some 5 us later than the order counts on, in a stage where the engines' order is fixed and VectorE cannot catch up. Delaying d6y alone in the kernel before showed this, with 1.96 us of stretch in its trace and 4.6 us by the medians. A chance of 0.22 was too little for it: the text itself called the cover thin.
- **The range** ended at 375.5 since it left out the far half of this rival; the 377.3 us that the rival gave for half of the idle time was the better bound. That it lies so near the measured 377.0 is luck, since it was worked out for the last tile's wait, and the last tile had none.
